# Reciprocals of softmax sums: spread by a row transpose and DRAM instead of by PE in two attention stages

## The chip, the cores and the metric

The kernel runs on one core of a Trainium2 chip. The metric is the device time of one execution in microseconds (us); before the change its median was 2735.3 us over three runs (2733.17 to 2743.01). The engines are PE (TensorE, matrix products and transposes; its weight loads are shown as PEld), DVE (VectorE), ACT (ScalarE), POOL (GpSimd) and SP (SyncE, which here issues the DMA transfers). Each takes its own instructions in order and waits on semaphores for the others. SBUF is the memory on the chip that all engines work on, PSUM is the memory of eight banks into which PE writes, DRAM is outside.

## The reference

The reference is one step of a two-layer encoder on a prompt of 2048 tokens and a sample of 64 more tokens with caches. Per layer:

```python
h = h + rms(mixed @ w_out) * g_post          # mixed: gated attention outputs
mixed = concat([o_a * silu(g_a), o_b * silu(g_b)])   # layer 0
mixed = o * silu(g)                                   # layer 1
```

`o_a` is latent attention over all earlier chunks. `o_b` is banded attention, eight heads of 64 numbers, each chunk of 64 tokens looking at itself and the eight chunks before it, with a bias by distance. `o` of layer 1 is banded attention with sixteen query heads and two key heads, each chunk looking at itself and two chunks before, with a sink per head. Every softmax is

```python
p = exp(s - max(s));  o = (p @ v) / sum(p)            # layer 1: sum(p) + exp(sink - max)
```

The kernel forms `p @ v` first and multiplies by the reciprocal of the sum afterwards. The change is about how that reciprocal gets to where it is multiplied.

## The kernel before

The attention output is held transposed: `OT` has one partition for each of the 64 numbers of two heads (128 partitions), and one column per token. The sums come out of the exponential's accumulator the other way: one partition per query token, one column per head. So each reciprocal, which stands in one partition per token, has to become a row that is repeated over 64 partitions.

Before, this is done with PE. The reciprocal tile `ri` is repeated 64 times along the free axis by a copy (`rb`, on ACT), and each 128x128 piece of `rb` is transposed by PE into a PSUM bank named `t` (a matmul against `ident`). DVE then multiplies `OT` by that bank, and POOL multiplies by the gate tile `G`, which was loaded from DRAM.

**Banded attention** (function `phase3`). Work units are (group of blocks, head, block): `GROUPS` is three groups of four blocks of 128 queries, then two groups of two. Between the units of the first group stand eight units for the sample. One call of `step(n)` does the exponential of the next unit, the scores of the one after (`unit(n + 2)`), and the transposes of the current one: `turn` transposes two or three 128x128 pieces of `P` into a `t` bank (two buffers in `ps_t`), ACT copies them out as `PT` and DVE forms the low part (`lo_of`). In between, matmuls of the output projection are put in as filler (`J.pump`, 1.9 k steps of three matmuls per step in the groups of four, from `RATE3`; 3.3 from `RATES`). When both heads of a pair are through a group, `finish` is added to the queue `J.side`: reciprocal, load of `G`, copy to `rb`, then two or three pauses (`YR3` is 3), transposes, two products, two pauses, and the store to `sMB`, from which later the tokens' tiles are read for the projection.

**Layer 1** (function `phase5`). Sixteen blocks of 128 queries (`BLOCKS5`), each of four units (key group g, half e). `step(n)` does the exponential of unit n+1, the scores of unit n+2, the transposes of unit n, the value products (`av`, into the single bank `acc`) and `out` of unit n-1, with `RATE5` = 4 k steps of projection as filler. With 4k as the first unit of a block, `out` of that unit is in step 4k+1. After a block's last unit, `out` computes the reciprocal and adds `gate` to `J.side`. `gate` loads `G`, spreads, transposes, multiplies, and makes the two parts of the projection's left operand (`MM`: a copy on ACT, a subtraction on POOL). It may not begin the `MM` of a tile while two tiles are made and not yet projected. `out` of a block's first unit turns a loop while two blocks are open, since `OT` has two buffers.

A generator in `J.side` moves on from one `yield` to the next when it is pumped: once per step (`J.rest`), in banded attention twice when two are queued, and in the loop of `out` once per turn. A pause is one such pump.

**Order.** From step 8 of layer 1 (`NAUTO5`) and step 4 of banded attention (`NAUTO3`), PE, DVE, ACT and SP take their instructions in the order in which the program writes them. POOL's order is chosen by the planner. A DMA that waits for its data holds every later DMA of SP.

The lines of the profile: L1202 transposes of P in banded attention, L1236 its reciprocal, L1245 the transposes of `rb`, L1246 and L1247 the two products; L1684 scores, L1705 transposes of P, L1712 value products, L1696, L1699 and L1700 exponentials, sink and sum of layer 1, L1734 the transposes of `rb`, L1736 and L1742 the products, L1749 the subtraction for `MM`, L1802 the sum of the two halves of `acc` into `OT`, L1806 the reciprocal; L963 the projection, L994 its scaling `z`, L1002 the residual; L211 and L214 are the helpers `copy` (ACT) and `lo_of` (DVE).

Of the kernel before, what the change touches and what calls it, by code (L numbers as in the profile page):

```python
# [7 lines left out]
F32 = mybir.dt.float32  # L8
# [3 lines left out]
ALU = mybir.AluOpType  # L12
# [98 lines left out]
def kernel(ctx, tc, a, o, upto=5):  # L111
# [11 lines left out]
    def scratch(name, shape):  # L123
        return dr.tile(shape, F32, name=name)
# [21 lines left out]

    sWO = [scratch(f"sWO{i}", [KT, 128, 2, DM]) for i in range(2)]
# [58 lines left out]
    def head_pair(dst, x, j, c0, w):  # L206

        return dst[x].rearrange("h d t -> (h d) t")[j * 128:j * 128 + 128, c0:c0 + w]

# [877 lines left out]
    def phase3():  # L1087
        with ExitStack() as st, ExitStack() as st_a:
# [60 lines left out]
            class Unit:  # L1149
# [42 lines left out]
                def turn(self, g):  # L1192
                    b0, nb = g
                    e = self.i % 2
                    if e == 0 and b0 == 0:
                        self.H.PT = PTs[turn[0] % NPT]
                        turn[0] += 1
                    PT = self.PT = self.H.PT
                    s0 = self.lo - self.base + self.off + b0
                    t = ps_t.tile([128, 4, 128], F32, name="t")  # L1200
                    for b in range(nb):
                        nc.tensor.transpose(t[:, b], self.P[:, (b0 + b) * 128:(b0 + b) * 128 + 128], ident)  # L1202
                    hi = PT[:, 0, s0:s0 + nb, e * 128:e * 128 + 128]
                    copy(hi, t[:, :nb])
                    return lambda: lo_of(PT[:, 1, s0:s0 + nb, e * 128:e * 128 + 128], t[:, :nb], hi)
# [24 lines left out]
            def finish(hp, OT, rs, b0, nb, last=False):  # L1230
# [4 lines left out]
                ri = sc.tile([128, 4, 2], F32, name="ri", bufs=2)  # L1235
                nc.vector.reciprocal(ri[:, :nb], rs[:, b0:b0 + nb])  # L1236
                G = ot.tile([128, 512], F32, name="G")
                dma(G[:, :n], sG[512 + hp * 128:640 + hp * 128, t0:t0 + n])
                rb = sc.tile([128, 4, 2, 64], F32, name="rb", bufs=1)
                copy(rb[:, :nb], ri[:, :nb, :, None].to_broadcast([128, nb, 2, 64]))  # L1240
                for _ in range(YR3 if t0 < 512 or t0 == SEQ else 2):
                    yield
                p = ps_t.tile([128, 512], F32, name="t")
                for b in range(nb):
                    nc.tensor.transpose(p[:, b * 128:b * 128 + 128], rb[:, b].rearrange("p a b -> p (a b)"), ident)  # L1245
                nc.vector.tensor_mul(OT[:, :n], OT[:, :n], p[:, :n])  # L1246
# [133 lines left out]
            W, us = [], {}  # L1380
# [265 lines left out]
    def phase5():  # L1646

        with ExitStack() as st:
# [7 lines left out]
            J.mm = None  # L1656
# [57 lines left out]
            def gate(OT, ri, t0, r):  # L1714

                G = qp.tile([128, 8, 128], F32, name="G")
                dma(G[:, :, :r], sGC[:, t0:t0 + r].rearrange("(j p) t -> p j t", p=128))
                rbs = []
                for g in range(2):
                    rb = sc.tile([128, 4, 2, 64], F32, name="rb", bufs=2)  # L1720
                    if r == 128:
                        copy(rb, ri[:, g].rearrange("p e c -> p c e")[:, :, :, None].to_broadcast([128, 4, 2, 64]))
                    else:
                        for e in range(2):
                            nc.gpsimd.tensor_copy(rb[:, :, e], ri[:, g, :, None].to_broadcast([128, 4, 64]))
                    rbs.append(rb)
                for _ in range(YRB if r == 128 else YRS):
                    yield
                for g in range(2):
                    t = ps_t.tile([128, 512], F32, name="t")  # L1730
                    tv = t.rearrange("p (j q) -> p j q", j=4)
                    js = slice(g * 4, g * 4 + 4)
                    for j in range(4):
                        nc.tensor.transpose(tv[:, j], rbs[g][:, j].rearrange("p e d -> p (e d)"), ident)  # L1734
                    if r == 128:
                        nc.vector.tensor_tensor(OT[:, js], OT[:, js], tv, op=ALU.mult)  # L1736
                    else:
                        for e in range(2):
                            er = slice(e * 64, e * 64 + 64)
                            nc.vector.tensor_tensor(OT[er, js, :r], OT[er, js, :r], tv[er, :, er], op=ALU.mult)  # L1740
                    yield
                nc.gpsimd.tensor_tensor(OT[:, :, :r], OT[:, :, :r], G[:, :, :r], op=ALU.mult)  # L1742
# [32 lines left out]
            class Unit(Soft):  # L1775
# [16 lines left out]
                def out(self):  # L1792
# [11 lines left out]
                    if (g, e) == (1, 1):  # L1804
                        ri = sc.tile([128, 2, 2, 4], F32, name="ri", bufs=2)
                        nc.vector.reciprocal(ri, B.rs)  # L1806
                        J.side.add(gate(B.OT, ri, B.i * 128, 128))

            def sample():
# [31 lines left out]
                ri = sc.tile([128, 2, 4], F32, name="ris", bufs=1)  # L1841
                nc.vector.reciprocal(ri, rs)
                J.side.add(gate(OT, ri, SEQ, DS))
# [32 lines left out]
            def step(n):  # L1876
# [25 lines left out]
                if n >= NS5:  # L1902
                    J.samp.pump(1)
                if J.made < FAST5:
                    J.side.pump(SP5)
# [4 lines left out]
            with manual(M5, ORDERED | {mybir.EngineType.SP}):  # L1910
# [3 lines left out]
                while J.done < 17:  # L1914
                    J.side.pump(TAIL)
# [110 lines left out]
```

## Time and profile before

| what | value |
|---|---|
| median of 3 runs | 2735.3 us |
| the profiled execution's own time | 2728.45 us |
| its span, and mean PE clock | 2726.7 us, 0.985 |
| PE, DVE, ACT, POOL busy over the span | 94%, 54%, 51%, 28% |
| transposes of `rb`: banded attention (L1245), layer 1 (L1734) | 68, 136 |
| their busy time on PE | 11.9 us, 20.5 us |
| spreads to `rb` on ACT in both stages | 56, 30.3 us |

In the views, a group of instructions is one line of the kernel, engine and operation, `out<-in`, shape, count, then busy time, mean duration in ns, idle time of the engine just before them and what ended it. The chain of waits runs back from the last instruction: at each step to what released it. A busy PE is not PE at its peak, since matmuls overlap.

### The profile page before, as it was taken

What the parts mean: (1) busy time and instruction counts of PE and PEld (TensorE: products, weight loads), DVE (VectorE), ACT (ScalarE), POOL (GpSimd) and SP (SyncE); (2) the same over time, 40 slices, a digit from 0 to 9 for tenths busy, and PEclk for the clock granted to TensorE, in tenths of its full rate; (3) what the DMA queues carried; (4) which work ended last, traced back from release to release, by engine and by line L of the source; (5) the groups of instructions that cost most, each with busy time, mean ns of one, the idle gap of its engine ahead of it and who ended that gap; (6) DMA issues with size and microseconds to landing.
All of it is one profiled execution on the core that took longest, in us unless ns stands there. A gap on an engine that the chain in (4) does not pass through costs nothing.

```text
span 2726.7 us, 46699 instructions
## 1 busy us (share of the span) xinstructions
PE 2565.9 (94%) x16296; PEld 2340.5 (86%) x16296; DVE 1471.5 (54%) x4050; ACT 1392.1 (51%) x3548; POOL 772.6 (28%) x1312
## 2 busy tenths in 40 slices
PE   6999999999999999999999999989999999999997
PEld 6999999899998888888777878769999998787886
DVE  5542235352127878787667666545113104787884
ACT  4332232333237777777666665552233224777783
POOL 2123122113112323321101323553113220344444
PEclk9999999999999999999899999999999999999999
DMA  6456443737537666661477676756525429455551
GB/s 236 160 155 213 124 150 97 249 110 228 165 95 210 183 180 188 170 165 55 169 202 187 179 187 172 205 187 216 155 99 166 128 70 250 109 139 134 136 132 70
DMA packets 382283, 437.92 MB, mean 161 GB/s; under 512 B 49937, under 2 KB 308889, under 8 KB 378817
## 3 DMA queue, kind: packets, MB, share of 16 engines
q1 hardware_dynamic: 382048, 434.95, 54.4%
q8 instruction: 129, 2.11, 0.3%
q14 instruction: 106, 0.86, 0.1%
HBM read 282.80 MB, written 157.09 MB: 161 GB/s over the span
## 4 chain that ended last, share of the span: by engine, by line
PE 73%; DVE 10%; ACT 6%; DMA 5%; issue 3%; POOL 2%; SPq 0%; ACTq 0%; DVEq 0%; POOLq 0%
PE pm L237 37%; PE proj L963 10%; PE s L682 6%; PE acc L753 4%; PE t L725 3%; DVE PT L214 2%; PE acc L1215 2%; PE t L1705 2%; PE acc L1712 2%; PE s L1175 2%; PE t L1202 1%; PE s L1684 1%; ACT P L701 1%; DVE m L688 1%; ACT PT L211 1%
## 5 line engine op out<-in xcount | busy, mean ns | idle before, releaser
L237 PE MATMUL pm<-X,W 128*128 128x384 f32 (+2 forms) x4536 | 753.4, 325 | 2.4 <-DVE ev L214 0.9
L237 PEld LDWEIGHTS pm<-X,W 128*128 128x128 f32 x4536 | 732.5, 190 | 5.5 <-DVE ev L214 1.1
L211 ACT ACTIVATE PT<-t 128x512 fp32r<-128x512 f32 (+3 forms) x704 | 344.6, 505 | 272.0 <-PE t L1202 120.4
L214 DVE SCALAR_TENSOR_TENSOR PT<-t,PT 128x512 fp32r<-128x512 f32 (+3 forms) x688 | 375.5, 569 | 105.2 <-ACT PT L211 103.4
L963 PE MATMUL proj<-Wo,MM 128*128 128x512 f32 (+1 forms) x1464 | 404.0, 406 | 18.1 <-ACT z L211 14.7
L228 POOL TENSOR_TENSOR W<-R,W 128x768 fp32r<-128x768 f32 (+3 forms) x114 | 230.4, 2048 | 534.0 <-ACT W L227 533.7
L214 DVE SCALAR_TENSOR_TENSOR ev<-pm,ev 128x256 fp32r<-128x256 f32 (+3 forms) x197 | 98.7, 503 | 467.3 <-ACT ev L1552 169.3
L963 PEld LDWEIGHTS proj<-Wo,MM 128*128 128x128 f32 (+1 forms) x1464 | 252.2, 186 | 68.8 <-ACT z L211 20.1
L237 PE MATMUL pm<-W,X 128*128 128x256 f32 (+5 forms) x2040 | 281.2, 297 | 0.0
L237 PEld LDWEIGHTS pm<-W,X 128*128 128x128 f32 (+1 forms) x2040 | 271.6, 187 | 1.4 <-POOL W L228 0.3
L701 ACT ACTIVATE P<-s,m 128x512 f32<-128x512 f32 (+9 forms) x344 | 209.5, 616 | 32.8 <-DVE m L690 30.5
L682 PE MATMUL s<-KA,Q 128*128 128x512 f32 (+7 forms) x640 | 201.1, 396 | 9.7 <-ACT P L701 8.8
L725 PE MATMUL t<-ident,P 128*128 128x128 f32 x1088 | 176.3, 276 | 3.4 <-ACT P L701 0.8
L688 DVE TENSOR_REDUCE m<-s 128x1 f32<-128x480 f32 (+7 forms) x216 | 132.4, 613 | 79.1 <-PE s L682 78.7
L725 PEld LDWEIGHTS t<-ident,P 128*128 128x128 f32 x1088 | 134.7, 141 | 41.5 <-ACT P L701 14.9
L753 PE MATMUL acc<-PT,V 128*128 128x256 f32 x1152 | 155.9, 285 | 6.6 <-DVE OT L762 6.6
L753 PEld LDWEIGHTS acc<-PT,V 128*128 128x128 f32 x1152 | 140.3, 188 | 12.0 <-PE t L725 6.0
L1696 ACT ACTIVATE P<-s,m 128x256 f32<-128x256 f32 (+2 forms) x264 | 119.7, 466 | 11.6 <-DVE m L1688 10.3
L1687 DVE CUSTOM_DVE_ANT_0 s<-s,mask 128x256 f32<-128x256 f32 (+1 forms) x256 | 107.7, 422 | 19.0 <-PE t L1705 8.1
L682 PE MATMUL s<-KR,Q 128*128 128x384 f32 (+6 forms) x320 | 116.3, 363 | 0.7 <-DMA Q<-sQR 0.7
L227 ACT ACTIVATE W<-R 128x768 fp32r<-128x768 f32 (+3 forms) x114 | 98.2, 910 | 36.5 <-DMA R<-in_ab_w_in_dram 18.2
L1179 DVE CUSTOM_DVE_ANT_0 s<-s,bias 128x640 f32<-128x640 f32 (+4 forms) x128 | 95.2, 744 | 38.6 <-PE s L1175 37.3
(249 smaller groups left out, 3961.0 us busy)
## 6 DMA issues: line engine op xcount, KB each, us to landing
Q<-sQA SPq DMA_DIRECT2D x128, 128.0 KB, 3.4
sWO<-W SPq DMA_DIRECT2D x32, 512.0 KB, 3.9
Q<-sQB SPq DMA_DIRECT2D x128, 128.0 KB, 3.5
Wo<-sWO SPq DMA_DIRECT2D x16, 1024.0 KB, 8.4
Q<-sQC SPq DMA_DIRECT2D x32, 512.0 KB, 7.6
R<-in_ab_w_in_dram SPq DMA_DIRECT2D x40, 384.0 KB, 3.5
K<-sKB SPq DMA_DIRECT2D x56, 256.0 KB, 5.0
V<-sVB SPq DMA_DIRECT2D x24, 512.0 KB, 6.2
```

The source lines that it names most:

```text
L211: nc.scalar.activation(out, in_, AF.Copy)
L214: nc.vector.scalar_tensor_tensor(out, x, scale, hi, op0=ALU.mult, op1=ALU.subtract)
L228: nc.gpsimd.tensor_tensor(Wv[:, 1, k0:k1], Rv, Wv[:, 0, k0:k1], op=ALU.subtract)
L237: nc.tensor.matmul(ps, lhs(x, k), rhs(y, k), start=(j == 0), stop=(j == n - 1))
L682: nc.tensor.matmul(s[:r, :n], self.Q[:, x, self.qo:self.qo + r], rhs, start=(x == 0), stop=(x == 2))
L688: nc.vector.tensor_reduce(m[:r, j:j + 1], s[:r, :n], axis=AX.X, op=ALU.max)
L701: nc.scalar.activation(self.P[:r, o0:o0 + n], self.s.pop(j)[:r, :n], AF.Exp, bias=self.m[:r, 6:7], accum_out=acc)
L725: nc.tensor.transpose(t[:, b], self.P[:, (b0 + b) * 128:(b0 + b + 1) * 128], ident)
L753: nc.tensor.matmul(acc[:, (i // 2) % 2], H.V[:, b0 + b], PT[:, x, b], start=(b0 + b == 0 and x == 0), stop=(b0 + b == i and x == 1))
L963: nc.tensor.matmul(p, M[:, x, k, :r], W[k][:, y, cs], start=(k == k0 and t == 0), stop=(k == k1 - 1 and t == 2))
L1687: nc.vector.tensor_tensor_reduce(s[:, c, :w], s[:, c, :w], mk, 1.0, -3e38, ALU.add, ALU.max, m[:, 0, c:c + 1])
L1696: nc.scalar.activation(self.P[:, c, :w], self.s[:, c, :w], AF.Exp, bias=m[:, 1, c:c + 1], accum_out=m[:, 0, c:c + 1])
```

## The change

Two stages get another way from `ri` to the rows. `to_rows` transposes the small tile `ri` itself (n columns of sums) by one PE transpose, so that each sum becomes a row of 128 tokens; ACT copies these n rows to SBUF and a DMA writes them to DRAM (`sRB`, `sRC`). `rows_to_halves` reads them back, each row repeated over 64 partitions, by two DMAs.

In banded attention this holds for the groups of four and the sample. The row transpose is handed to a list `rows`, and the next `turn` with fewer than four pieces does it in the free quarter of its own `t` bank. Groups of two keep the old way (the order of the spread's axes is changed only in the view). In layer 1 the reciprocal moves to the step in which the block's last unit gets its exponentials (`sums`), a separate queue `J.recips`, moved on once a step, does the row transpose in a `t` bank, the write, the read and POOL's product of `G` by `rb`; `gate` then has one DVE product of `OT` by that.

```diff
+    sRB = scratch("sRB", [4, 6, 8, 128])
+    sRC = scratch("sRC", [17, 16, 128])
...
+    def to_rows(pool, p, ri, n, dst):
+        nc.tensor.transpose(p[:n], ri, ident)
+        e = pool.tile([16, 128], F32, name="rT", bufs=1)
+        nc.scalar.activation(e[:n], p[:n], AF.Copy)
+        dma(dst, e[:n])
+
+    def rows_to_halves(out, src, half, ap):
+        for e in range(2):
+            dma(out[e * 64:e * 64 + 64], bass.AP(tensor=src.tensor, offset=src.offset + e * half, ap=[[0, 64]] + ap))
...
                         nc.tensor.transpose(t[:, b], self.P[:, (b0 + b) * 128:(b0 + b) * 128 + 128], ident)
+                    if rows and nb < 4:
+                        to_rows(sc, t[:, 3], *rows.pop(0).args)
...
-                ri = sc.tile([128, 4, 2], F32, name="ri", bufs=2)
-                nc.vector.reciprocal(ri[:, :nb], rs[:, b0:b0 + nb])
+                ri = sc.tile([128, 8], F32, name="ri", bufs=2)
+                nc.vector.reciprocal(ri[:, :2 * nb].rearrange("p (e b) -> p e b", e=2),
+                                     rs[:, b0:b0 + nb].rearrange("p b e -> p e b"))
...
-                rb = sc.tile([128, 4, 2, 64], F32, name="rb", bufs=1)
-                copy(rb[:, :nb], ri[:, :nb, :, None].to_broadcast([128, nb, 2, 64]))
-                for _ in range(YR3 if t0 < 512 or t0 == SEQ else 2):
+                rb = sc.tile([128, 512], F32, name="rb", bufs=1)
+                if nb == 2:
...
+                else:
+                    sr = sRB[hp, -(-t0 // 512), 0:2 * nb]
+                    task = K()
+                    task.args = ri[:, :2 * nb], 2 * nb, sr
+                    rows.append(task)
                     yield
-                p = ps_t.tile([128, 512], F32, name="t")
-                for b in range(nb):
-                    nc.tensor.transpose(p[:, b * 128:b * 128 + 128], rb[:, b].rearrange("p a b -> p (a b)"), ident)
-                nc.vector.tensor_mul(OT[:, :n], OT[:, :n], p[:, :n])
+                    while task in rows:
+                        yield
+                    yield
+                    rows_to_halves(rb[:, :n], sr, nb * 128, [[1, n]])
+                    yield
+                    yield
+                    yield
+                    nc.vector.tensor_mul(OT[:, :n], OT[:, :n], rb[:, :n])
                 nc.gpsimd.tensor_tensor(OT[:, :n], OT[:, :n], G[:, :n], op=ALU.mult)
...
-            def gate(OT, ri, t0, r):
-                G = qp.tile([128, 8, 128], F32, name="G")
-                dma(G[:, :, :r], sGC[:, t0:t0 + r].rearrange("(j p) t -> p j t", p=128))
-                rbs = []
...
+            def recips(ri, i, R):
+                n = ri.shape[-1]
+                r = 128 if i < 16 else DS
+                to_rows(sc, ps_t.tile([128, 512], F32, name="t")[:, :128], ri, n, sRC[i, :n])
+                yield
+                rb = sc.tile([128, 8, 128], F32, name="rb", bufs=1)[:, :, :r]
+                rows_to_halves(rb, sRC[i], 8 * 128 if r == 128 else 64, [[128, 8], [1, r]])
+                R.G = qp.tile([128, 8, 128], F32, name="G")[:, :, :r]
+                dma(R.G, sGC[:, i * 128:i * 128 + r].rearrange("(j p) t -> p j t", p=128))
+                yield
+                yield
+                nc.gpsimd.tensor_tensor(R.G, R.G, rb, op=ALU.mult)
+                R.made = True
+                yield
+
+            def gate(OT, R, t0, r):
+                while not R.made:
                     yield
-                for g in range(2):
-                    t = ps_t.tile([128, 512], F32, name="t")
...
-                nc.gpsimd.tensor_tensor(OT[:, :, :r], OT[:, :, :r], G[:, :, :r], op=ALU.mult)
+                yield
+                nc.vector.tensor_tensor(OT, OT, R.G, op=ALU.mult)
                 while J.made - J.done >= 2 or not J.mm:
                     yield
...
-                        ri = sc.tile([128, 2, 2, 4], F32, name="ri", bufs=2)
-                        nc.vector.reciprocal(ri, B.rs)
-                        J.side.add(gate(B.OT, ri, B.i * 128, 128))
+                        J.side.add(gate(B.OT, B.R, B.i * 128, 128))
+                def sums(self):
+                    B = self.B
+                    ri = sc.tile([128, 16], F32, name="ri", bufs=2)
+                    nc.vector.reciprocal(ri.rearrange("p (e g c) -> p g e c", e=2, g=2), B.rs)
+                    B.R = K()
+                    B.R.made = False
+                    J.recips.add(recips(ri, B.i, B.R))
...
+                R = K()
+                R.made = False
+                yield
+                yield from recips(ri, 16, R)
+                J.side.add(gate(OT, R, SEQ, DS))
...
+                J.recips.each()
+                if nxt and (nxt.g, nxt.e) == (1, 1):
+                    nxt.sums()
                 if J.made < FAST5:
                     J.side.pump(SP5)
                 J.rest()
...
                 while J.done < 17:
+                    J.recips.each()
                     J.side.pump(TAIL)
```

More of the change, by code (lines that the diff above doesn't have):

```diff
@@ new lines, in finish @@
+                if nb == 2:
+                    rv = rb.rearrange("p (b e d) -> p e b d", e=2, d=64)[:, :, :nb]
+                    copy(rv, ri[:, :2 * nb].rearrange("p (e b) -> p e b", e=2)[:, :, :, None].to_broadcast([128, 2, nb, 64]))
+                    for _ in range(YR3):
+                        yield
+                    p = ps_t.tile([128, 512], F32, name="t")
+                    for b in range(nb):
+                        nc.tensor.transpose(p[:, b * 128:b * 128 + 128], rb[:, b * 128:b * 128 + 128], ident)
+                    nc.vector.tensor_mul(OT[:, :n], OT[:, :n], p[:, :n])
+                else:
[3 more added lines that the diff above has]
+                    rows.append(task)
+                    yield
+                    while task in rows:
[6 more added lines that the diff above has]
+                    nc.vector.tensor_mul(OT[:, :n], OT[:, :n], rb[:, :n])
@@ L1379, in phase3 @@
             load_values(*loads[0])
-            W, us = [], {}
+            W, us, rows = [], {}, []
             for n in range(LC):
@@ L1655, in phase5 @@
             J.open = 0
-            J.mm = None
+            J.mm, J.recips = None, Fill()
             mask = one.tile([128, 256], F32, name="mask")
@@ L1712, in values @@
                     nc.tensor.matmul(acc, V, PT[:kk, x], start=(first and x == 0), stop=(last and x == 1))
-            def gate(OT, ri, t0, r):
-                G = qp.tile([128, 8, 128], F32, name="G")
-                dma(G[:, :, :r], sGC[:, t0:t0 + r].rearrange("(j p) t -> p j t", p=128))
-                rbs = []
-                for g in range(2):
[L1720 to L1727, printed above, removed]
-                    yield
-                for g in range(2):
-                    t = ps_t.tile([128, 512], F32, name="t")
[L1731 to L1742, printed above, removed]
@@ L1840, in sample @@
                     yield
-                ri = sc.tile([128, 2, 4], F32, name="ris", bufs=1)
-                nc.vector.reciprocal(ri, rs)
-                J.side.add(gate(OT, ri, SEQ, DS))
+                ri = sc.tile([128, 8], F32, name="ris", bufs=1)
+                nc.vector.reciprocal(ri, rs.rearrange("p g c -> p (g c)"))
+                R = K()
+                R.made = False
+                yield
+                yield from recips(ri, 16, R)
+                J.side.add(gate(OT, R, SEQ, DS))
             units = [(i, g, e) for i in range(16) for g in range(2) for e in range(2)]
```

## The prediction

> **What bounds the kernel now.** I read, in this order, the page's head, the busy time by stretch, the chain of waits of layer 1, one of its blocks in order of time, and then who waits in the two places that the diff touches.
>
> The head, and the stretches 1340 to 1800 us (banded attention) and 2300 to 2690 us (layer 1's attention); the columns are length, then busy time with instruction counts of PE, PEld, DVE, ACT and POOL, PE clock, DMA share and GB/s:
>
> ```profile
> span 2726.7 us, 46699 instructions
> PE 2565.9 (94%) x16296; PEld 2340.5 (86%) x16296; DVE 1471.5 (54%) x4050; ACT 1392.1 (51%) x3548; POOL 772.6 (28%) x1312
> 1340.00:1800.00 460.00, 424.71 (x2612) 359.38 (x2613) 288.75 (x791) 277.50 (x705) 127.79 (x249) 0.97 0.70 191
> 2300.00:2690.00 390.00, 363.17 (x2071) 301.45 (x2071) 319.32 (x855) 293.49 (x878) 167.57 (x369) 0.99 0.51 130
> ```
>
> PE is busy 92% and 93% of the two stretches, DVE 63% and 82%. PE sets the pace, and in layer 1 DVE is not far behind.
>
> One block of layer 1, from its chain of waits (start, length, work):
>
> ```profile
> 2431.74 2.10 PE proj L963 x9
> ...
> 2441.87 0.44 PE t L1734 x4
> ...
> 2446.72 0.45 PE t L1705 x4
> ...
> 2447.83 0.69 DVE PT L214
> 2448.52 0.90 DVE z L994 x2
> 2449.42 2.51 issue
> 2451.93 0.67 DVE OT L1802
> ...
> 2454.78 0.61 DVE PT L214
> 2455.39 0.04 issue
> 2455.43 0.66 PE t L1705 x4
> 2456.09 2.10 PE proj L963 x9
> ```
>
> A block takes 2456.09 - 2431.74 = 24.35 us, so one of its four steps about 6.1. Four transposes of spread reciprocals cost PE 0.44 us of its path, 0.11 each (their mean duration, below, is latency in a pipeline). Nine projection matmuls take 2.10, 0.233 each. Once a block the chain leaves PE for DVE. The same moment in order of time, with what ended the idle time in brackets:
>
> ```profile
> 2444.04 0.63 DVE L1736 TENSOR_TENSOR OT<-OT,t 128x512 f32<-128x512 f32 x1
> 2444.75 2.39 POOL L1742 TENSOR_TENSOR OT<-OT,G 128x1024 f32<-128x1024 f32 x1 [4.18 <-DVE OT L1736]
> 2444.96 0.22 ACT L1699 ACTIVATE m<-m 128x4 f32<-128x4 f32 x1
> 2447.10 0.20 POOL L1700 TENSOR_TENSOR rsum<-m 128x4 f32<-128x4 f32 x1
> 2447.69 1.05 ACT L211 ACTIVATE MM<-OT 128x1024 fp32r<-128x1024 f32 x1
> 2448.44 3.57 DVE L994 SCALAR_TENSOR_TENSOR z<-z,rs,g_post 128x512 f32<-128x512 f32 x2
> 2448.82 2.64 POOL L1749 TENSOR_TENSOR MM<-OT,MM 128x1024 fp32r<-128x1024 f32 x1 [1.37 <-ACT MM L211]
> 2452.75 1.16 PE L1712 MATMUL acc<-PT,VC 128*128 128x512 f32 x4 [0.72 <-DVE OT L1802]
> ```
>
> PE idles 0.72 us here, because DVE adds to OT (L1802) late: the two z products take 3.57 us, and the second ends at 2452.01, 0.55 us after POOL's subtraction (2448.82 + 2.64 = 2451.46), which also has to release OT. Note that a POOL product held the small sum L1700 from 2445.18 (the end of L1699) to 2447.10: this returns as a risk.
>
> **Layer 1, part by part.** Groups of the whole run (busy, mean ns, idle before):
>
> ```profile
> L1734 PE MATMUL t<-ident,rb 128*128 128x128 f32 x136 | 20.5, 274 | 1.8 <-DVE PT L214 1.4 <-DVE OTs L1740 0.2 <-ACT rb L211 0.2
> L1736 DVE TENSOR_TENSOR OT<-OT,t 128x512 f32<-128x512 f32 x32 | 20.8, 653 | 3.0 <-PE t L1734 2.9
> L211 ACT ACTIVATE rb<-ri 128x512 f32<-128x512 f32 (+2 forms) x56 | 30.3, 570 | 17.9 <-DVE ri L1236 17.1 <-PE t L1245 0.8
> L263 DVE SCALAR_TENSOR_TENSOR R<-R,rs,g_pre 128x1024 f32<-128x1024 f32 (+1 forms) x34 | 43.4, 1327 | 0.6
> L211 ACT ACTIVATE e<-po 128x128 f32<-128x128 f32 (+1 forms) x20 | 4.9, 280 | 10.3 <-PE po L502 8.1 <-DMA out_dram<-e 2.1
> PE acc L1712 <- DVE OT L1802: 14.5, 16, 3.8
> ```
>
> (The last is from PE's waits of 2300 to 2727 us: total, times, longest.)
>
> (1) PE. 136 transposes go (8 for each of 16 blocks and 8 for the sample), 17 row transposes come, at 0.11 us each: -15.0 + 1.9 = -13.1 us. The 1.8 us that L1734 waited for a bank goes too, since one bank is asked for instead of two, while the step's earlier one is free: -1.8. This lies on PE's path.
> (2) ACT, DVE, POOL. ACT loses two spreads (570 ns) and gains one copy of 16 rows (at most the 280 ns of e<-po): -0.9 us a block, off the path. DVE loses two products from PSUM (653 ns each) and gains one of 128x1024 from SBUF; L263, the same width with both inputs in SBUF, took 1327 ns: even. POOL keeps one 128x1024 product, now G by rb.
> (3) DRAM. The row is written at the end of step 4k+3, read back a step later with G, multiplied by POOL two steps after that and used by DVE at the end of the next step 4k+3. Nearest rows for landing (KB, median us; the first two from 2340 to 2660 us, the others from 1370 to 1460):
>
> ```profile
> G<-sGC SPq DMA_DIRECT2D x14, 512.0 KB, 8.6
> out_dram<-x SPq DMA_DIRECT2D x11, 512.0 KB, 2.6
> sMB<-OTs SPq DMA_DIRECT2D x4, 32.0 KB, 3.1
> G<-sG SPq DMA_DIRECT2D x4, 256.0 KB, 3.9
> ```
>
> Write 2.6 to 3.1 us against one step of 6.1: covered. Loads 3.9 to 8.6 us, plus issue of two more DMAs, against two steps of 12.2: covered, and the cover beyond that is one step. SP stands at the row write until ACT's copy, and VC, x and output transfers queue behind it; they are wanted steps later, so nothing. G's load moves two steps forward, ahead of the next block's KC and Q transfers instead of behind them; that can only help it.
> (4) Order. Following the generators through the pumps: the old gate takes six pumps a block, but four steps give four, so the loop in `out` turned twice (POOL's OT by G and the MM copy both there). The new one needs four, but then waits for the projections, so the loop turns once, for the MM copy alone. The second z product falls into the next step, behind L1802. L1802 then waits for the subtraction alone, some 0.47 us earlier (2451.93 against 2451.46); PE has one k step (three matmuls, 0.7 us) more or less to fill the gap. Bounds for the 14.5 us of acc waits: all gone, or 0.7 us more in each of 16 blocks (+11). I take -4, since 16 x 0.47 is 7.5 and the filler may take part of it.
> (5) The new waits. The reciprocal moves one unit earlier, into the step of its own exponentials: DVE, and behind it the next reductions and PT, stands if POOL's sum is late. In the quoted row it was 1.9 us late, but DVE gets there only after two PT copies, which ACT makes after the same exponentials. Bounds 0 and 16 x 2.4 = 38 us; I take 0.25 us a block, +4.
> (6) Tail. POOL's product no longer lies between the last products and the last MM:
>
> ```profile
> 2693.96 5.32 PE L963 MATMUL proj<-Wo,MM 128*128 128x512 f32 x22 [1.48 <-POOL MM L1749]
> ```
>
> -1.5 (0 to -2.4). By my count five k steps (3.5 us) move from the blocks to the tail; PE does them in either place, 0.
>
> Layer 1: -13.1 - 1.8 - 4 + 4 - 1.5 = -16.4 us.
>
> [...]
>
> **Banded attention.**
>
> ```profile
> PE t L1245 <- DVE PT L214: 8.6, 9, 1.8
> L1245 PE MATMUL t<-ident,rb 128*128 128x128 f32 x68 | 11.9, 281 | 9.1 <-DVE PT L214 9.1
> L1236 DVE RECIPROCAL ri<-rss x4: 146/148/149, 1367.0 to 1451.8; 128x2 f32<-128x2 f32 x4
> ```
>
> (The first is from the waits of 1340 to 1560 us, the first two groups of four.) 52 transposes go (12 x 4 and the sample's 4), 16 row transposes come, in the free quarter of a bank that the unit holds anyway: -36 x 0.11 = -4.0 us. The 8.6 us that PE stood for a bank of its own lies nearly all at edited places; all may go or none, and I take -6, because the next transposes may find DVE late as well. The unit's own copy is delayed by a copy of 8 rows, at most 0.28 us, 16 times, behind PE's other work: 0 (to +4). ACT loses a spread per finish for it, DVE's product reads SBUF instead of PSUM at the same width, and the groups of two keep their old way with the axes of the spread in another order: nothing.
>
> In the first group finishes of heads and of the sample alternate and the queue is pumped twice a step, so DVE's product comes three steps after the row transpose. Sample reciprocals come every ten steps: (1451.8 - 1367.0)/30 = 2.83 us a step, 8.5 us for copy, write (3.1), two issues and load (3.9): about even. A miss stops DVE, and PE by the next bank. Bounds 0 and eight times 4 us; I take 0.5 each, +4. Later groups have more time. Tokens become ready four steps later, which by my count leaves seven k steps (4.9 us) to the end of the stage; the steps without filler are shorter by as much, of which I leave +2.
>
> Banded attention: -4 - 6 + 4 + 2 = -4 us.
>
> **Sum.** -20.4 us. The profiled execution took 2728.45 us (span 2726.7), 6.9 below the median shown; it would become 2708, and the median 2735.3 - 20 = 2715.
>
> **Rivals.** (A) No difference to be told: new order and DVE's waits eat most. For it: DVE at 82% in layer 1, and 13.1 + 4.0 us of PE's work is only 17. If (4) and bank waits give nothing and (5) takes 0.5 us a block (8), -17 + 8 + 4 + 2 = -3: 2732. (B) Slower: POOL's queue. It is not held to the written order, and a product of G by rb that is put at POOL's head before its data has landed holds L1689 and L1700 behind it, then ACT's exponential of the sinks and DVE's reciprocal. With G landing 8.6 us after an issue of up to 2 us and POOL there after one step of 6.1, that is 4 us in each of 16 blocks, +64, of which the slack of one step hides perhaps a third: +43 - 20 = +23, 2758. It decides from 1.3 us a block on PE's path (16 x 1.3 = 20). Against: two steps lie between. [...] (D) More gain: all acc and bank waits go and no new ones come, -13.1 - 1.8 - 14.5 - 1.5 - 4 - 8.6 = -43: 2692. (E) That the rows don't do what the diff says I give nothing: both orders of e and b are written out.
>
> **How the numbers follow.** Forecast 0.52, A 0.24, B 0.08, C 0.08, D 0.08. A measurement of this kernel tells about 0.5%, 13.7 us, from no change. Faster by more: most of the forecast (0.48 of it), D, a little of A: 0.58. Slower by more: B and a part of C and of A's other side: 0.14. Within: 0.28. The forecast's own range is 2701 to 2726; for eight in ten it reaches to D's upper half and to C: 2698 to 2741.
>
> **What would show it.** Right: no group of eight transposes in a block, period near 23.2 to 23.5 us; acc waits near 10 us; no wait on t in the first groups; row copies of some 0.25 us. Wrong: DVE idle before the reciprocal or before its product with G (step 5, rivals B and C), POOL idle for G, ACT's sink exponential late; in the first group DVE idle for rb over 1 us a time; a longer stage end after 1800 us. If the period stays at 24.35, PE did not set it.

## The result, and the profile after

The kernel after took 2797.3 us (median of 4 runs, 2793.07 to 2801.73), the kernel before beside it 2737.3 us. The ratio is 1.022, with a 95% interval of 1.020 to 1.024: some 60 us slower, where 20 us faster was forecast and 2741 us was the upper end of the range.

The head of the page, and below it two stretches; columns as for the kernel before:

```profile
span 2791.3 us, 46626 instructions
...
PE 2578.8 (92%) x16141; PEld 2349.1 (84%) x16141; DVE 1443.9 (52%) x4031; ACT 1371.9 (49%) x3533; POOL 769.5 (28%) x1308
```

```profile
1340.00:1800.00 460.00, 414.65 (x2543) 350.32 (x2544) 286.59 (x790) 271.86 (x702) 126.68 (x241) 0.97 0.72 195
2300.00:2690.00 390.00, 328.44 (x1730) 271.58 (x1730) 262.24 (x754) 247.03 (x776) 138.57 (x306) 0.90 0.56 138
```

PE has 155 instructions less and yet 12.9 us more busy time. The 155 are the 119 of layer 1 and the 36 of banded attention that the forecast counted. In banded attention PE is busy 10 us less. In layer 1 it is busy 84% of the stretch instead of 93%, and its clock is 0.90 instead of 0.99.

One row measures the stretch of layer 1 that matters: the copies of `acc` (ACT's `tbm`), four for each of the 16 blocks, with min, median and max in ns, then the start of the first and of the last. First the kernel before, then the one after:

```profile
L211 ACT ACTIVATE tbm<-acc x64: 581/595/600, 2289.7 to 2683.5; 64x512 f32<-64x512 f32 x64
```

```profile
L226 ACT ACTIVATE tbm<-acc x64: 581/596/600, 2291.7 to 2748.1; 64x512 f32<-64x512 f32 x64
```

From first to last these are 393.8 us before and 456.4 us after: +62.6 us. It starts 2.0 us later, and after the last copy both kernels need 43 us to the end of the span (2726.7 - 2683.5, 2791.3 - 2748.1). So all of the loss lies between these copies. Below, "the stretch" is this difference.

Who waits there, from the waits of 2300 to 2760 us (total, times, longest):

```profile
DVE OT L1830 <- POOL MM L1777: 72.8, 12, 7.1
PE acc L1746 <- DVE OT L1830: 64.6, 16, 6.1
POOL G L1761 <- DMA G<-sGC: 34.9, 10, 4.1
```

PE's waits for `acc` went from 14.5 us to 64.6. The bank is held because DVE cannot add into `OT` (L1830), and DVE waits for POOL's subtraction (L1777), which is the last reader of the `OT` of the block two before: there are two buffers, and the new block takes that one. One such moment in the chain of waits:

```profile
2540.58 7.19 DMA G<-sGC
...
2547.94 2.35 POOL G L1761
2550.28 2.31 POOL MM L1777
...
2552.61 0.69 DVE OT L1830
...
2553.44 2.04 PE acc L1746 x4
...
2561.32 0.92 PE acc L1746 x4
```

And the same in order of time, with the idle time before an instruction in brackets:

```profile
2540.58 0.54 SPq L1758 DMA_DIRECT2D G<-sGC  x1
...
2544.26 0.20 POOL L1723 TENSOR_TENSOR m<-m,sink 128x4 f32<-128x4 f32 x1 [0.30 <-DVE m L1722]
...
2545.26 1.05 ACT L226 ACTIVATE MM<-OT 128x1024 fp32r<-128x1024 f32 x1
...
2547.93 2.35 POOL L1761 TENSOR_TENSOR G<-G,rb 128x1024 f32<-128x1024 f32 x1 [3.47 <-PE s L1718]
...
2550.23 2.35 POOL L1777 TENSOR_TENSOR MM<-OT,MM 128x1024 fp32r<-128x1024 f32 x1
...
2552.61 0.68 DVE L1830 TENSOR_TENSOR OT<-acc,tbm 64x512 f32<-64x512 f32 x1 [6.52 <-POOL MM L1777]
...
2553.44 2.04 PE L1746 MATMUL acc<-PT,VC 128*128 128x512 f32 x4 [5.23 <-DVE OT L1830]
```

POOL's next instruction after 2544.46 is the product of `G` by `rb` for the next block. It stands 3.47 us: `G` was asked for at 2540.58 and took 7.19 us. (The bracket names PE's scores, which by the profile ended at the same moment, 2547.77; the product reads nothing of theirs, and the chain names the transfer.) Under all names in such brackets POOL stood 60.8 us ahead of this product in the whole run, 34.9 of them under `G`'s own name. The subtraction, whose input from ACT was ready at 2546.31, begins at 2550.23, 3.9 us later. Then DVE, then PE with 5.23 us idle. The program writes the subtraction in step 4k+1 and the product in step 4k+2; the planner put them on POOL the other way round:

```
POOL's order in the kernel after:   ... m (L1723), G<-G,rb (L1761), MM<-OT,MM (L1777), ...
POOL's order as written (e3):       ... MM<-OT,MM (L1777), ..., m (L1723), G<-G,rb (L1761), ...
```

### The profile page after: what moved, and what is told of

Same layout as the page of the kernel before. It is cut to its first block, busy times and chain, and to the rows that moved or that the text cites. A ratio compares the mean times of both kernels' runs of the same rounds, so it can differ in the third digit from the quotient of the medians.

```text
span 2791.3 us, 46626 instructions
## 1 busy us (share of the span) xinstructions
PE 2578.8 (92%) x16141; PEld 2349.1 (84%) x16141; DVE 1443.9 (52%) x4031; ACT 1371.9 (49%) x3533; POOL 769.5 (28%) x1308
## 4 chain that ended last, share of the span: by engine, by line
PE 71%; DVE 9%; DMA 9%; ACT 5%; POOL 3%; issue 2%; SPq 1%; POOLq 0%; ACTq 0%; DVEq 0%
PE pm L252 37%; PE proj L978 9%; PE s L697 6%; PE acc L768 4%; PE t L740 3%; DMA G<-sGC 2%; PE acc L1746 2%; PE acc L1232 2%; DVE PT L229 2%; PE t L1217 1%; PE s L1190 1%; PE t L1739 1%; ACT P L716 1%; PE s L1718 1%; DVE m L703 1%
## 5 line engine op out<-in xcount | busy, mean ns | idle before, releaser
L768 PE MATMUL acc<-PT,V 128*128 128x256 f32 x1152 | 155.9, 285 | 6.5 <-DVE OT L777 6.5
L1746 PE MATMUL acc<-PT,VC 128*128 128x512 f32 x248 | 84.9, 464 | 68.1 <-DVE OT L1830 64.6
L1730 ACT ACTIVATE P<-s,m 128x256 f32<-128x256 f32 (+2 forms) x264 | 119.1, 462 | 12.9 <-DVE m L1722 11.8
L1746 PEld LDWEIGHTS acc<-PT,VC 128*128 128x128 f32 x248 | 51.8, 219 | 84.8 <-issue 64.6
L1232 PE MATMUL acc<-PT,V 128*128 128x256 f32 x672 | 113.2, 301 | 6.3 <-DVE OT L1242 5.5
```

Of the source, the lines that this page charges most:

```text
L768: nc.tensor.matmul(acc[:, (i // 2) % 2], H.V[:, b0 + b], PT[:, x, b], start=(b0 + b == 0 and x == 0), stop=(b0 + b == i and x == 1))
L1232: nc.tensor.matmul(acc, self.H.V[:, self.base - self.H.b0 + b], self.PT[:, x, off + b], start=(b == 0 and x == 0), stop=(b == nblk - 1 and ...
L1746: nc.tensor.matmul(acc, V, PT[:kk, x], start=(first and x == 0), stop=(last and x == 1))
```

## The experiments

Ratios are to the kernel before, run beside each on the same chip (medians there 2731 to 2734 us), with 95% intervals. All kernels started from the one after unless another is named.

**e1, e2: which part.** e1 has the banded part of the change alone, e2 the part in layer 1 alone.

> Only banded attention's part of the change; layer 1 is the kernel before. Theory (the loss lies in layer 1): 2735 to 2745 us, the stage 2 to 5 us longer than before, with DVE idle for rb some 17 us in all. Rival (the row way costs as much in both stages): 2755 to 2770 us.

> Only layer 1's part; banded attention is the kernel before. Theory: nearly the whole loss, 2788 to 2800 us, block period 28.2 us, DVE's sum into OT idle for POOL's subtraction some 70 us. Rival (the two parts share the loss): 2760 to 2775 us.

e1: 2733.2 us, 1.0007 [0.9993, 1.0021], a little under the range expected. e2: 2791.6 us, 1.0223 [1.0192, 1.0254], as expected. The whole loss is layer 1's. The banded part makes no difference that shows in the time.

**e3, e4: POOL's order.** e3 takes POOL's instructions in the written order in layer 1; nothing else differs. e4 does that to the kernel before, as a control.

```diff
-            with manual(M5, ORDERED | {mybir.EngineType.SP}):
+            with manual(M5, ORDERED | {mybir.EngineType.SP, mybir.EngineType.Pool}):
```

> The whole change, with POOL too held to the written order in layer 1 from step 8; nothing else on any engine is different. So POOL's product of G by rb comes behind the subtraction for MM instead of ahead of it. Theory (the product stands at POOL's head until G has landed, and the subtraction that releases OT stands behind it): OT's wait for the subtraction falls from 73 us to under 25, period 23.5 to 24.5 us, 2720 to 2745 us. [...]

> The kernel before, with POOL held to the written order in layer 1 in the same way: the control for e3. Theory: within 10 us of before, 2728 to 2748 us, so that what e3 gains is not the order's own gain. Rival (the written order is good or bad by itself): more than 15 us off.

e3: 2732.3 us, 1.0001 [0.9990, 1.0013]; the stretch is 390.1 us. The order of one engine took back the 60 us. e4: 2755.5 us, 1.0088 [1.0060, 1.0117]; against the expectation, the written order costs the kernel before 22 us, so what e3 regains isn't a gain that this order brings to any kernel. The waits of e3, 2300 to 2700 us, and then of e4:

```profile
POOL rsum L1734 <- ACT m L1733: 60.1, 31, 6.7
DVE OT L1830 <- POOL MM L1777: 35.6, 12, 5.6
PE acc L1746 <- DVE OT L1830: 24.8, 16, 3.6
...
POOL G L1761 <- DMA G<-sGC: 3.0, 1, 3.0
```

```profile
POOL rsum L1700 <- ACT m L1699: 104.3, 31, 5.7
DVE OT L1802 <- POOL MM L1749: 34.0, 13, 4.8
PE acc L1712 <- DVE OT L1802: 29.7, 16, 4.3
```

In e3 POOL hardly waits for `G` any more, but DVE's wait for the subtraction is 35.6 us where less than 25 was expected. In e4 POOL stands 104.3 us at the small sums for ACT, against 44.2 in the kernel before, and DVE's wait for the subtraction is 34.0 us against 9.4. That the one makes the other is argued and not shown: in e3 POOL stands 60.1 us at the sums, less than the 100.0 of the kernel after. In both, `OT` is released by POOL; the next kernels take that away.

**e5: OT released by DVE.** The planner's order stays; the product is written into `G`'s tile, and ACT's copy and POOL's subtraction read that. POOL may stand as before, but `OT` doesn't wait for it.

```diff
-                nc.vector.tensor_tensor(OT, OT, R.G, op=ALU.mult)
+                nc.vector.tensor_tensor(R.G, OT, R.G, op=ALU.mult)
...
-                copy(MM[:, 0, :, :r], OT[:, :, :r])
-                nc.gpsimd.tensor_tensor(MM[:, 1, :, :r], OT[:, :, :r], MM[:, 0, :, :r], op=ALU.subtract)
+                copy(MM[:, 0, :, :r], R.G)
+                nc.gpsimd.tensor_tensor(MM[:, 1, :, :r], R.G, MM[:, 0, :, :r], op=ALU.subtract)
```

> The whole change, POOL in the planner's order, but DVE's product of OT and G is written into the tile of G, and MM is made from there. OT is then released by DVE's product, a step before the subtraction, which no longer stands between a block's OT and the one after next. The order on PE, ACT, DVE and SP stays. Theory (the loss is OT waiting for a subtraction that stands behind the late product of G by rb): DVE's sum into OT waits under 10 us in all, period 23.0 to 24.0 us, 2710 to 2735 us. Rival (a late POOL holds DVE and ACT by other ways too, by the sums and the sink's m): the waits move there, 2760 us or more.

e5: 2722.4 us, 0.9976 [0.9965, 0.9986]; stretch 385.6 us. Its waits of 2300 to 2700 us:

```profile
POOL G L1761 <- DMA G<-sGC: 45.6, 12, 5.8
...
PE acc L1746 <- DVE OT L1830: 8.4, 6, 4.0
```

POOL stands ahead of the product as long as in the kernel after (63.2 us under all names against 60.8), and still ahead of the subtraction, but PE's wait is down from 64.6 to 8.4 us. That joins e3: the loss needs both POOL standing for the transfer and `OT` behind it.

**e6: the transfer earlier.** `G`'s tile and its load come one step earlier, ahead of the row transpose.

```diff
+                R.G = qp.tile([128, 8, 128], F32, name="G")[:, :, :r]
+                dma(R.G, sGC[:, i * 128:i * 128 + r].rearrange("(j p) t -> p j t", p=128))
                 to_rows(sc, ps_t.tile([128, 512], F32, name="t")[:, :128], ri, n, sRC[i, :n])
...
-                R.G = qp.tile([128, 8, 128], F32, name="G")[:, :, :r]
-                dma(R.G, sGC[:, i * 128:i * 128 + r].rearrange("(j p) t -> p j t", p=128))
```

> The whole change, with G's load written ahead of the row transpose and the row's write, so that SP issues it without standing at the row. Theory: G lands in time, POOL then waits for rb only, which lands about 2 us before G did; with the planner's order kept, 2755 to 2780 us; if the planner also puts the product behind the subtraction, 2730 to 2745 us. Rival (G's lateness is not what holds POOL): 2790 us or more.

e6: 2764.1 us, 1.0126 [1.0110, 1.0142]; stretch 430.7 us. Its waits, 2300 to 2725 us:

```profile
DVE OT L1830 <- POOL MM L1777: 56.5, 12, 6.4
PE acc L1746 <- DVE OT L1830: 47.4, 16, 6.0
POOL G L1761 <- DMA rb<-sRC: 29.6, 8, 7.9
```

About two fifths of the loss goes (25.7 of the 62.6 us). POOL now stands for `rb`, the row that comes back from DRAM, which was hidden behind `G` until then.

**e7: the banded load earlier.** e1 with `rb`'s load one pause earlier and the product where it was.

```diff
-                    yield
                     rows_to_halves(rb[:, :n], sr, nb * 128, [[1, n]])
                     yield
                     yield
                     yield
+                    yield
```

> Banded attention's part alone, as in e1, with rb loaded one pause earlier after the row transpose and the product at the same pause as before. Theory (DVE's 17 us wait for rb takes back what PE gained): that wait falls below 6 us and the time to 2722 to 2730 us. Rival (the wait is covered, or SP only stands at the write one step longer): 2730 to 2738 us, as e1.

e7: 2731.8 us, 1.0007 [0.9993, 1.0021], as e1. DVE's waits for `rb` nearly stayed: in 1340 to 1560 us 11.8 us for `OT` in both, and 3.5 for the sample's against 5.1. The load stands earlier in the order, but in the kernel after, whose banded part is e1's, SP already stands at it until the row's write has landed (39.5 us in the same time), so it started about as early as the row allowed.

**e8: several repairs together.** e5 with `G` as in e6 and the banded load as in e7; and `OT` counts as free from the product on, so that the loop in `out` doesn't turn.

```diff
                 nc.vector.tensor_tensor(R.G, OT, R.G, op=ALU.mult)
+                J.open -= r == 128
...
-                J.open -= r == 128
                 for _ in range(DRDY):
```

> The whole change with the three edits together: product into G's tile with a block closed at that product, so that the loop in out does not turn; G's load ahead of the row; rb of banded attention one pause earlier. POOL in the planner's order. Theory: 2700 to 2720 us, period 23.0 to 23.5 us. Rival (the loop's extra projection work was needed, or POOL's order strikes elsewhere): 2730 us or more.

e8: 2749.6 us, 1.0070 [1.0057, 1.0082]: worse than e5 by 27 us. Waits of 2300 to 2700 us:

```profile
POOL G L1761 <- DMA rb<-sRC: 66.9, 14, 6.4
...
PE t L1739 <- DVE PT L229: 25.5, 16, 3.3
DVE rs L190 <- POOL rs L189: 19.5, 11, 3.8
```

POOL stands again, now for `rb`, and another victim is behind it: its share of the norm's inverse root (L189), for which DVE waits, and behind DVE the low parts of `PT`, and PE. This resembles rival B, with the norm's small work in the place of the sums. Which of the three edits brought it was not separated; in the written order, below, an early `G` does no harm.

**e9, e10: e5 with POOL in the written order**, e10 with `G` as in e6 too.

> The kernel of e5 (OT released by VectorE's product) with GpSimd in the written order in layer 1; only the order of GpSimd's instructions differs from e5. Theory: once OT is no longer released by GpSimd, GpSimd's order matters little, and its 45.6 us of waiting for G shrink: 2710 to 2722 us. Rival: the written order costs by itself, as the 22 us that it cost in the kernel before, and the time is 2735 us or more.

> e9 with the load of G issued one step earlier, ahead of the row. Theory: in the written order the product of G by rb stands behind the subtraction, so an earlier G changes nothing that anything waits for: within 5 us of e9. Rival: GpSimd in the written order still stands for G, and without that the time is 5 us or more below e9.

e9: 2717.7 us, 0.9947 [0.9929, 0.9964]; stretch 374.8 us. e10: 2717.1 us, 0.9941 [0.9925, 0.9958]: no difference to e9. A block of e9 in order of time:

```profile
2541.20 2.42 POOL L1777 TENSOR_TENSOR MM<-G,MM 128x1024 fp32r<-128x1024 f32 x1 [1.95 <-ACT MM L226]
2541.77 0.68 DVE L1830 TENSOR_TENSOR OT<-acc,tbm 64x512 f32<-64x512 f32 x1 [0.88 <-ACT tbm L226]
2542.77 1.18 PE L1746 MATMUL acc<-PT,VC 128*128 128x512 f32 x4
...
2546.57 2.42 POOL L1761 TENSOR_TENSOR G<-G,rb 128x1024 f32<-128x1024 f32 x1
```

The subtraction stands ahead of the product, DVE's addition doesn't wait for either, PE runs through, and the product waits for nothing.

**e11, e13: without the rows.** e11 is the kernel before with POOL's product written into `G`'s tile, in the way of e5; e13 is that in POOL's written order.

```diff
-                nc.gpsimd.tensor_tensor(OT[:, :, :r], OT[:, :, :r], G[:, :, :r], op=ALU.mult)
+                nc.gpsimd.tensor_tensor(G[:, :, :r], OT[:, :, :r], G[:, :, :r], op=ALU.mult)
```

> The kernel before, with GpSimd's product of OT and G written into G's buffer, and ScalarE's copy and the subtraction read from there: OT is free after that product. No row, no DRAM. It tells whether the 9 us by which e5 beats the kernel before come from the release of OT alone. Theory: half or less of them do, since in the kernel before the addition into OT waits little for the subtraction: 2726 to 2732 us. Rival: all of them do: 2718 to 2725 us, and the rows bring nothing at all.

> The kernel of e11 (no rows; OT released by the product into G's buffer) with GpSimd in the written order in layer 1. Theory: the rows have a gain of their own in layer 1 once nothing stands behind a transfer, and this kernel is 5 us or more slower than e9: 2722 us or more (in the written order GpSimd's own product by G still stands behind VectorE's two products). Rival: all of e9's gain is that of the release and the order: 2713 to 2721 us, as e9.

e11: 2726.2 us, 0.9975 [0.9965, 0.9985]. Its median is in the theory's range, but its ratio is e5's (0.9976): in the planner's order the whole change brings nothing beside the release. e13: 2739.4 us, 1.0019 [1.0008, 1.0030]; on that chip e9 again (e15) took 2721.1 us, and e14 (below), which like e13 has the old banded part, 2712.7. So in the written order the whole change brings 18 us and the rows in layer 1 alone 26.7. Row of the copies for e11, e13 and e9:

```profile
L211 ACT ACTIVATE tbm<-acc x64: 580/595/599, 2290.7 to 2678.9; 64x512 f32<-64x512 f32 x64
```

```profile
L211 ACT ACTIVATE tbm<-acc x64: 580/594/599, 2296.6 to 2698.8; 64x512 f32<-64x512 f32 x64
```

```profile
L226 ACT ACTIVATE tbm<-acc x64: 581/596/600, 2294.9 to 2669.7; 64x512 f32<-64x512 f32 x64
```

The stretches are 388.2, 402.2 and 374.8 us. Without the rows POOL's large product needs DVE's product just ahead of it and, in the written order, takes its place in the chain of waits (7.9% of e13's chain between 2300 and 2690 us; e9's product of `G` by `rb` has 1.6%). With the rows it needs only transfers, and in the written order most have landed: in e9 it waits 10.9 us for them in all.

**e12: the banded part without its wait.** In the groups of four, `OT` is multiplied by the gate's tile a second time instead of by `rb`, so the division by the sums is left out there.

```diff
-                    nc.vector.tensor_mul(OT[:, :n], OT[:, :n], rb[:, :n])
+                    nc.vector.tensor_mul(OT[:, :n], OT[:, :n], G[:, :n])
```

> The banded part alone (as e1), but the groups of four multiply OT by the gate's tile instead of by the tile of reciprocals: the row, its write and its loads are still issued, but nothing waits for them. It leaves out the division by the sums in these groups. Theory: VectorE's 16.8 us of waits for rb are what eats the 10 us of work that TensorE lost in this stage: 2722 to 2727 us. Rival: the waits were idle time that cost nothing, and something else bounds the stage: within 3 us of e1 (2729 to 2735 us).

e12: 2725.6 us, 0.9979 [0.9967, 0.9991], in the theory's range and 7.6 us under e1 (the two intervals lie apart). So the waits for `rb` do cost. The waits of 1340 to 1560 us, first of e1, then of e12:

```profile
DVE OT L1280 <- DMA rb<-sRB: 11.8, 4, 3.9
PE t L1217 <- DVE PT L229: 11.0, 6, 4.2
```

```profile
PE s L1190 <- DMA K<-sKB: 8.6, 4, 3.3
...
PE t L1217 <- DVE PT L229: 2.3, 4, 1.0
```

With DVE's wait for `rb` gone, PE's wait for DVE's low parts falls from 11.0 to 2.3 us: DVE, standing for the row, held them. In this execution PE waits 8.6 us for keys instead (0.6 in e1), and its own time, 2730.6 us, is 4.9 us above the median, so the trace shows little of the gain.

**e14, e15: the best version with and without the banded part.** e14 is e9 with the banded part of the kernel before, e15 is e9 once more.

> e9 with the banded part of the kernel before. Theory: the banded part of the change makes no difference here either (e1): within 4 us of e9. Rival: its end 3.4 us later costs that here: 5 us or more below e9.

> The kernel of e9 once more, on the same chip as e13 and e14, so that they can be compared with it without the kernel before between them. Theory: 2712 to 2722 us, a ratio to the kernel before of 0.993 to 0.997. Rival: e9's gain was that of its chip, and this run is within 0.2% of the kernel before.

e14: 2712.7 us, 0.9923 [0.9908, 0.9938], the fastest of all. e15: 2721.1 us, 0.9958 [0.9945, 0.9971]. So in this company the banded part costs 8.4 us on that chip, the rival's answer. Whether by a later end of the stage, as that rival had it, one trace of each can't tell: the stretch in layer 1 starts at 2294.4 us in e14 and 2301.1 in e15, but at 2294.9 in e9, which is the same kernel as e15. Where the 8.4 us come from stays open.

| kernel | stretch in layer 1, us | ratio to before |
|---|---|---|
| before | 393.8 | 1 |
| after | 456.4 | 1.0222 |
| e4, before with POOL as written | 416.9 | 1.0088 |
| e8, several repairs | 407.7 | 1.0070 |
| e6, G earlier | 430.7 | 1.0126 |
| e3, POOL as written | 390.1 | 1.0001 |
| e5, OT released by DVE | 385.6 | 0.9976 |
| e11, release without rows | 388.2 | 0.9975 |
| e13, e11 with POOL as written | 402.2 | 1.0019 |
| e9, e15, both repairs | 374.8, 380.1 | 0.9947, 0.9958 |
| e14, e9 without the banded part | 375.9 | 0.9923 |

## Why the prediction was wrong

**Step (3), the step that failed.** It took the loads to be covered by "two steps of 12.2" us. That counts from issue to use in the written order, and POOL isn't held to it. In the block shown, POOL stood at the product 3.9 us after `G`'s issue (2540.58 to 2544.46), not 12.2. The landing time was near in that block: 7.19 us against the 8.6 taken. The other half of the step, "SP stands at the row write ... so nothing", hid the same thing. From SP's own waits of 2300 to 2760 us:

```profile
SPq L218 <- ACT rT L217: 258.8, 16, 24.0
```

SP stands at the row write for 16 us a block, so the loads behind it cannot be issued ahead of their step. e6 shows that `G`'s issue time was only a part of it: with `G` early, `rb` was the late one. Its landing, and that of banded attention's `rb`, lie at or under the bounds of the forecast, 3.9 to 8.6 us for a load (KB, median us, whole run), so it was not the size of the transfers that was wrong:

```profile
rb<-sRC SPq DMA_DIRECT2D x32, 256.0 KB, 6.2
rb<-sRB SPq DMA_DIRECT2D x24, 128.0 KB, 3.1
```

**Step (4), the wrong sign.** It said that L1802 would wait "for the subtraction alone, some 0.47 us earlier", and bounded the acc waits by +11 us. They grew by 50.1 us (64.6 - 14.5), because the subtraction itself came late, 3.9 us in the block shown. The wait was seen and its releaser was named; what could stand ahead of that releaser on POOL was not asked.

**Rival B** had the cause, with a chance of 0.08. It had the product at POOL's head and the 4 us a block (3.47 measured in the block shown). Its victim was wrong: not the small sums, but the subtraction that frees `OT`. So the price was wrong too: the sums have a step of slack, of which it gave a third back, and `OT` with two buffers has none: of the 60.8 us that POOL stood ahead of the product most reached PE (its waits grew by 50.1), and the clock came on top (0.90 in the stretch, 0.99 before). It forecast 2758 us. Of its signs, "POOL idle for G" came; DVE's product waited for POOL's only once (10.9 us, in the first block).

**Steps (2), (5) and (6).** The groups of the whole run after (busy, mean ns, idle before):

```profile
L1770 DVE TENSOR_TENSOR OT<-OT,G 128x1024 f32<-128x1024 f32 x16 | 19.4, 1210 | 10.9 <-POOL G L1761 10.9
L217 ACT ACTIVATE rT<-t 16x128 f32<-16x128 f32 (+2 forms) x33 | 8.8, 266 | 12.4 <-PE t L215 11.0 <-DMA sRC<-rT 1.3
L1839 DVE RECIPROCAL ri<-rsum 128x16 f32<-128x16 f32 x16 | 4.0, 253 | 1.9 <-POOL rsum L1734 1.4
```

ACT's row copies took 266 ns (at most 280 forecast). DVE's product took 1210 ns, less than the 1327 of the nearest row, and all 16 of its runs lie between 1205 and 1226 ns. (In e9 it took 1203 to 1698 ns, with a median of 1204.) In the trace no large POOL product stands beside any of the 16, so rival C (0.08), in which the new product meets one, is out. No run shows the time that this rival put on top; what the kernel before shows of such a meeting is `z`: its products have a median of 744 ns, and the one that starts at 2449.10, while the subtraction runs (2448.82 to 2451.46), took 2.91 us. DVE's new idle time before the reciprocal, step (5), was 1.9 us, where +4 was taken. Of step (6) the wait is gone from PE's waits as forecast, but no gain shows: from the last copy to the end it is 43.2 us in both kernels.

**The forecast of layer 1, -16.4 us,** lies near what e9, e14 and e15 reach (stretch -19.0, -17.9 and -13.7), but that is luck and no support for its terms. In e14 it is the sum of the release of `OT` (-5.6, e11), of what the written order costs without the rows (+14.0, e13 against e11) and of what the rows bring in that order (-26.3, e14 against e13). The forecast has neither of the first two, which are no part of the change, and the third is not its -16.4. In the planner's order the stretch is only 2.6 us shorter with the rows than with the release alone (e5 against e11).

**Banded attention, -4 us.** Measured: no difference (e1). PE's busy time in the stretch fell by 10 us (424.71 to 414.65), but the stage did not end earlier. The stores of its output, first in the kernel before and then in e1 (start of the first and of the last at the end):

```profile
L1250 SPq DMA_DIRECT2D sMB<-OT x20: 319/332/383, 1388.9 to 1799.0; - x20
```

```profile
L1284 SPq DMA_DIRECT2D sMB<-OT x20: 320/332/613, 1399.3 to 1802.8; - x20
```

In the six traces with the old banded part the last store starts at 1796.7 to 1806.1 us, in the eight with the changed one as it stands at 1802.4 to 1811.9. That DVE's waits for `rb` ate the gain rests on e12's times; its one trace has the last store no earlier, at 1806.8. The waits, shown under e12, are close to 3 us a time, where 0.5 was taken and 4 was the bound. And the forecast's own doubt came true ("the next transposes may find DVE late as well"): PE's 8.6 us of waits at the edited place became 11.0 us at the transposes of `P`. The terms mis-sized are these two, the +4 for `rb` and the -6 for bank waits, whose bound of none is what came. A product that comes more steps after the load wasn't tried, nor a third buffer of `OT` in layer 1; both are open.

## What to carry to other kernels

Where an engine's order is chosen by a planner, the cover of a transfer is not the distance in the written program: ask what can be put behind the first instruction that waits for it, and whether any of that frees a buffer. Before a product is moved ahead of its old place on a shared engine, look at what else releases the accumulator, and let an engine that waits for no transfer do it. An order has no worth of its own: the written one cost the kernel before 22 us, took back the loss of the kernel after, and brought some 5 us between e5 and e9. A repair of one late input may only uncover the next (`rb` behind `G`) or the next victim (the norm behind `OT`), so it is worth measuring alone.

## What the runs showed of the hardware

PE lost more than the time in which it stood. Stretches around the gap shown above, in the kernel after (PE's clock is the third number from the end):

```profile
2547.00:2553.00 6.00, 1.21 (x11) 0.97 (x9) 0.39 (x1) 2.96 (x11) 4.81 (x3) 1.00 1.07 228
2553.00:2556.00 3.00, 2.56 (x9) 2.10 (x9) 2.86 (x11) 0.00 (x0) 0.00 (x0) 0.50 0.02 5
2561.00:2572.00 11.00, 11.00 (x66) 9.46 (x65) 9.32 (x27) 8.62 (x28) 3.97 (x16) 1.00 0.41 128
```

After 5.23 us without work the granted clock was 0.50 for about 3 us, and four value products took 2.04 us in the chain, against 0.92 for four at full clock 8 us later. In the kernel before, the gap was 0.72 us, the clock 1.00 in the time behind it (2453 to 2456) and 0.99 in the whole stretch. An estimate of what this cost: PE's busy time rose by 12.9 us over the run although by the forecast's count 13.1 + 4.0 us of its work had gone, so its work took some 30 us longer, beside the 50.1 us of added waiting. (50.1 + 12.9 = 63.0, near the 62.6 us by which the stretch grew.) This was in no part of the forecast. How long PE has to stand for such a drop was not shown.
